# Stick-breaking and sliding-window units in turns of two: one layer of a hybrid decoder

## The chip, the cores and the metric

The kernel runs on one core of one Trainium2 chip. The metric is the device time of one execution in microseconds. Before the change it is 1794.3 us, the median of 3 runs (1792.6 to 1796.31). The profile comes from one further execution of the same program.

## The reference

One layer over 1024 positions with a model width of 2048. A pre-norm, one input projection to 6656 columns, two groups of attention heads side by side, and one output projection:

```
u = rmsnorm(x, norm_pre)
q_sb, k_sb, v_sb, z_sb, q_sw, k_sw, v_sw, z_sw = split(u @ w_in)
# stick-breaking, 16 heads of 64, s < t:
w[t,s] = sigmoid(l[t,s]) * prod_{s<j<t} (1 - sigmoid(l[t,j]));   l = q.k / 8
# sliding window of 128, 16 query heads on 4 key/value heads, bias by distance, one sink logit per head:
p = softmax over the window and the sink
y = concat(rmsnorm(o_sb) * silu(z_sb), rmsnorm(o_sw) * silu(z_sw)) @ w_out
out = x + rmsnorm(y, norm_post)
```

Everything is float32. The kernel keeps that precision by splitting an operand into a rounded part and a remainder ("h" and "l" in the names) and adding up two or three matmuls.

## The kernel before

The input projection is cut into 52 blocks of 128 columns. Three of them are computed while x is loaded; the others follow in the order of the list `work`, each by `proj`: 16 contraction tiles, three matmuls of 128x512 per tile and half of the positions, 96 "long" matmuls in a block (tiles p_..., line 122). The weights of a block come in four parts (`split_w`, lines 128 to 136): a load, a rounding on ScalarE (whi) and a subtraction on VectorE (wlo), one part ahead of its use.

The attention is cut into units, which are put between the long matmuls. After every three long matmuls of a contraction tile `proj` calls `step`, and `advance` decides whether something of a unit is issued. A unit has three stages on TensorE, all "small" matmuls:

- s1: the logits, four matmuls of 128x256 into a bank of PSUM (tile z_..., two buffers). ScalarE, GpSimd and VectorE then make the weights: for a stick-breaking unit two sigmoids (lines 555 and 557), two scans (565 or 568) and a product (571) into b_sb; for a sliding-window unit bias, maximum, exponentials, sum and scaling (639 to 654) into L_sw.
- s2: up to four 128x128 transposes of these weights (tile wt_..., line 126, two buffers), which ScalarE rounds (wh_..., lines 586 and 665) and VectorE subtracts (wl_..., 587 and 666).
- s3: up to four matmuls of 128x256 with the values (tile o_...). There is one PSUM buffer for it (`po`, lines 91 and 92). ScalarE copies a finished output to ot_... (line 518), from where it is stored.

A pair of stick-breaking heads (names sb0 to sb7) has 20 units, ten a head: query blocks a = 0 to 3, and for each the key blocks c = a to 3, which add up into one output; only the unit with c = 3 is followed by a copy. A group of sliding-window heads (sw0 to sw3) has 16 units, and each has an output and a copy of its own. In the names, sb2_0_1_3 is pair 2, head 0, a = 1, c = 3; sw1_5_0 is group 1, block 5, first two heads.

`pe_time` adds up the nominal time of all matmuls issued so far. Units wait in `todo` until a period has passed since the last start (4.7 or 3.8 us); a unit's s2 is due 6.2 or 7.0 us after its s1 was issued, its s3 4.5 or 5.0 us after its s2. When a period has passed, `advance` issues, in this order: all outputs that are due, one start (s1), and one s2; s2 goes ahead of the start where three units are already begun. When no unit is left to start, outputs and transposes are issued one by one as they come due. The order of TensorE's instructions is kept as the program writes it; the order on the other engines comes from a scheduler.

When a block of values is finished (`done_vsw`, `done_v_sb`), `drain` forces all units of earlier heads that use the value tiles, then `evac_v` takes two value tiles (tag "v", two buffers) and puts off the transposes of the values (vt_..., line 414) by 4 or 9 us; the next head's units are offered 6 us later.

After the attention the output projection runs as seven products of half-size matrices with sums (lines 935 to 994), in which no unit takes part.

Of the kernel before, what the change touches and what calls it, by code (L numbers as in the profile page):

```python
# [12 lines left out]
F32R = mybir.dt.float32r  # L13
# [6 lines left out]
P = 128  # L20
# [37 lines left out]
def layer(ctx, tc, xT, x, w_first, w_blk, w_out, g_pre, g_post, g_sb, g_sw, sinks, rel, onehot, penalty, out):  # L58
# [29 lines left out]
    def pw(name, shape=None):  # L88
        return ptile("pw", name, 2, shape)
# [62 lines left out]
    def advance(force=False):  # L152
        now = pe_time[0]
        while waiting and (force or waiting[0][0] <= now):
            todo.extend(waiting.pop(0)[1])
            prep()
        if later and (force or later[0][0] <= now):
            later.pop(0)[1]()
            return True
        if force or not todo:  # L160
            return finish_stage2(force, now) or finish_stage1(force, now) or (bool(todo) and start(now))
        if len(stage1) - stage1_due(now) < todo[0]["depth"] and last_start[0] + todo[0]["period"] <= now:
            while finish_stage2(False, now):
                pass
            late = len(stage1) >= todo[0]["depth"]
            if late:
                finish_stage1(False, now)
            begun = start(now)
            if not late:
                finish_stage1(False, now)  # L170
            return begun
        return False

    def start(now):
# [8 lines left out]
        prep()  # L183
        return True

    def stage1_due(now):
        return 1 if stage1 and len(stage2) < 3 and stage1[0][0] + stage1[0][1]["lag"] <= now else 0

    def finish_stage2(force, now):
        if stage2 and (force or stage2[0][0] + stage2[0][1]["lag2"] <= now):  # L190
            u = stage2.pop(0)[1]
# [3 lines left out]
        return False  # L195

    def finish_stage1(force, now):
        if stage1 and len(stage2) < 3 and (force or stage1_due(now)):
# [325 lines left out]
    def units_sb(pair, vst):  # L524
        units = []
        for hh in range(2):
            row = hh * HD
            head = {}
            for a in range(4):
                grp = {}  # L530
                for c in range(a, 4):
                    units.append(unit_sb(pair, hh, row, a, c, head, grp, vst[hh]))
        return units

    def unit_sb(pair, hh, row, a, c, head, grp, vs):
        nm = f"sb{pair}_{hh}_{a}"
        un = f"{nm}_{c}"
        me = {}
# [51 lines left out]
        def s3():  # L590
            if c == a:
                grp["o"] = po(f"o_{nm}")
            for j in range(2):
                for i, wt in enumerate(me["wt"]):
                    mm(grp["o"][:, :256], vs[:, 2 * c + j, :], wt[:, 2 - 2 * j:4 - 2 * j, :],
                       start=(c == a and j == 0 and i == 0), stop=(c == 3 and j == 1 and i == 1))
            if c == 3:
                finish_o(grp["o"], nm, pair, row, slice(a * 256, (a + 1) * 256))
# [10 lines left out]
    def unit_sw(g, i, hp, head, vg):  # L609
# [59 lines left out]
        def s3():  # L669
            ops = po(f"o_{un}")  # L670
            for j in range(nj):
                for r, wt in enumerate(me["wt"]):
                    mm(ops[:, :256], vg[:, i + j, :], wt[:, j, :],
                       start=(j == 0 and r == 0), stop=(j == nj - 1 and r == 1))
            finish_o(ops, un, 8 + blk, None, slice(i * P, (i + 1) * P))

# [14 lines left out]

    def done_vsw(i):
        def f(ps):
            for g in range(2 * i):
                drain(f"sw{g}")
            vs["sw", 2 * i], vs["sw", 2 * i + 1] = evac_v(ps, f"vsw{i}", 4.0 if i else 9.0)
        return f

    def done_q_sb(p):
# [4 lines left out]

    def done_v_sb(p):
        def f(ps):
            for g in range(4):
                drain(f"sw{g}")
# [332 lines left out]
```

## Time and profile before

| | |
|---|---|
| median of 3 runs | 1794.3 us (1792.6 to 1796.31) |
| the profiled execution's own time | 1794.37 us |
| its span, first to last instruction | 1792.5 us |
| mean granted clock of TensorE | 0.998 |
| TensorE matmuls (PE), busy | 1770.6 us, 9046 instructions |
| VectorE (DVE), busy | 1230.5 us |
| ScalarE (ACT), busy | 784.4 us |
| GpSimd (POOL), busy | 497.2 us |

PE is TensorE, PEld its weight loads, SP the engine that issues most DMAs. Times are microseconds unless marked ns. In a row of the timeline stand the start, the length, the engine, the line and operation, out<-in by the program's names without numbers, and the shapes; in brackets the idle time before it and what ended it. In a row of the waits stand the waiting engine, its tile and line, what it waited for, and then the sum, the number of waits and the longest. In a row of the groups stand the count (x...), the busy time, the mean length in ns, and the idle time before them with what ended it. Matmuls overlap and their ends are modelled, so their starts tell more than their lengths.

### The profile page before, as it was taken

The page shows a single profiled execution, that of the slowest core. Times are in us where ns is not written, and L with a number is a line of the kernel's source. Part 1 is how long each engine was busy: PE and PEld are TensorE (multiplying, and loading weights), DVE is VectorE, ACT ScalarE, POOL GpSimd, SP SyncE. Part 2 cuts the span into 40 slices and gives each one's busy share as a digit, 9 for nine tenths or more (in the row PEclk, how much of TensorE's full clock was granted, in tenths as well). Part 3 has the DMA queues.
Part 4 walks back from the last instruction along what each step waited for, and adds up shares of the span by engine and source line. Part 5 has one row for each costly group of instructions (what it writes and reads, how often), then busy time and mean ns, then how long its engine had stood idle before and what let it go on. Part 6 is the DMA issues. An engine that isn't in the chain of part 4 may idle for free. (4 is left out here: it accounts for less than half of the span.)

```text
span 1792.5 us, 27351 instructions
## 1 busy us (share of the span) xinstructions
PE 1770.6 (99%) x9046; PEld 1500.1 (84%) x9046; DVE 1230.5 (69%) x1984; ACT 784.4 (44%) x1696; POOL 497.2 (28%) x648
## 2 busy tenths in 40 slices
PE   8999999999999999999999999999999999999998
PEld 7788888888888888888888888888888887888886
DVE  7567842678367688675785777767868646855795
ACT  7345531456344444343443444444434434444442
POOL 0012121211213334233233332232313224504533
PEclk9999999999999999999999999999999999999999
DMA  7557775566746656556456563454434385634484
GB/s 232 191 162 212 211 223 158 163 205 204 222 134 182 181 168 190 162 182 183 156 166 178 177 181 124 154 164 142 146 106 136 103 256 190 210 100 140 136 286 155
DMA packets 203884, 312.48 MB, mean 174 GB/s; under 512 B 24640, under 2 KB 84192, under 8 KB 203616
## 3 DMA queue, kind: packets, MB, share of 16 engines
q1 hardware_dynamic: 201680, 307.60, 55.8%
q10 hardware_dynamic: 2064, 3.15, 0.5%
q8 instruction: 72, 1.18, 0.3%
q14 instruction: 68, 0.56, 0.1%
HBM read 219.42 MB, written 91.23 MB: 173 GB/s over the span
## 5 line engine op out<-in xcount | busy, mean ns | idle before, releaser
L587 DVE TENSOR_TENSOR wl_sb<-wt_sb,wh_sb 128x512 fp32r<-128x512 f32 (+1 forms) x160 | 100.7, 633 | 95.8 <-ACT wh_sb L586 95.8
L571 DVE TENSOR_TENSOR b_sb<-b_sb,m_sb 128x512 f32<-128x512 f32 x160 | 129.2, 807 | 42.1 <-POOL b_sb L561 19.1
L586 ACT CAST wh_sb<-wt_sb 128x512 fp32r<-128x512 f32 (+1 forms) x160 | 87.0, 544 | 136.3 <-PE wt_sb L126 134.3
L568 DVE TENSOR_TENSOR_SCAN m_sb<-m_sb,m_sb,zero 128x257 f32<-128x257 f32 x192 | 143.4, 785 | 2.4 <-ACT m_sb L555 2.1
L933 PE MATMUL y<-wohi,x 128*128 128x512 f32 x448 | 141.9, 393 | 1.5 <-ACT wohi L797 1.5
L933 PE MATMUL y<-wohl,x 128*128 128x512 f32 x576 | 132.5, 389 | 0.0
L933 PEld LDWEIGHTS y<-wohl,x 128*128 128x128 f32 x576 | 108.1, 188 | 22.4
L565 DVE TENSOR_TENSOR_SCAN m_sb<-m_sb,mask 128x256 f32<-128x256 f32 x128 | 119.8, 972 | 5.8 <-ACT m_sb L555 5.8
L648 ACT ACTIVATE L_sw<-L_sw,nm_sw 128x256 f32<-128x256 f32 (+1 forms) x128 | 63.1, 494 | 93.1 <-DVE nm_sw L643 91.7
L122 PE MATMUL p_vsb<-xh,whi_vsb 128*128 128x512 f32 x256 | 102.0, 398 | 0.0
L933 PEld LDWEIGHTS y<-wohi,x 128*128 128x128 f32 x448 | 84.9, 189 | 19.9 <-ACT wohi L797 1.9
L122 PE MATMUL p_ksb<-xh,wlo_ksb 128*128 128x512 f32 x256 | 100.7, 393 | 0.0
L122 PE MATMUL p_qsb<-xh,whi_qsb 128*128 128x512 f32 x256 | 100.6, 393 | 0.0
L122 PE MATMUL p_zsw<-xh,wlo_zsw 128*128 128x512 f32 x256 | 100.6, 393 | 0.0
L122 PE MATMUL p_qsb<-xh,wlo_qsb 128*128 128x512 f32 x256 | 100.6, 393 | 0.0
L122 PE MATMUL p_vsb<-xh,wlo_vsb 128*128 128x512 f32 x256 | 100.5, 393 | 0.0
L122 PE MATMUL p_ksb<-xl,whi_ksb 128*128 128x512 f32 x256 | 100.5, 392 | 0.0
L122 PE MATMUL p_vsb<-xl,whi_vsb 128*128 128x512 f32 x256 | 100.4, 392 | 0.0
L122 PE MATMUL p_qsb<-xl,whi_qsb 128*128 128x512 f32 x256 | 100.4, 392 | 0.0
L122 PE MATMUL p_zsw<-xl,whi_zsw 128*128 128x512 f32 x256 | 100.4, 392 | 0.0
L122 PE MATMUL p_zsb<-xh,wlo_zsb 128*128 128x512 f32 x256 | 100.4, 392 | 0.0
L122 PE MATMUL p_zsb<-xl,whi_zsb 128*128 128x512 f32 x256 | 100.2, 391 | 0.0
(243 smaller groups left out, 4988.3 us busy)
## 6 DMA issues: line engine op xcount, KB each, us to landing
row_sw<-in_w_out SPq DMA_DIRECT2D x80, 256.0 KB, 4.3
bg<-in_w_out SPq DMA_DIRECT2D x80, 256.0 KB, 4.3
woraw<-wsum SPq DMA_DIRECT2D x80, 256.0 KB, 3.4
kh<-kd SPq DMA_DIRECT2D x160, 64.0 KB, 2.9
kl<-kd SPq DMA_DIRECT2D x160, 64.0 KB, 2.4
wsum<-row_sw SPq DMA_DIRECT2D x40, 256.0 KB, 2.9
wsum<-bg SPq DMA_DIRECT2D x40, 256.0 KB, 3.3
q_sw<-qd SPq DMA_DIRECT2D x64, 128.0 KB, 3.5
```

Source lines behind the costliest of these rows:

```text
L122: tc.keep_in_program_order(nc.tensor.matmul(ps, a, b, start=start, stop=stop))
L565: nc.vector.tensor_tensor_scan(m[:, tb, 1:257], m[:, tb, 1:257], mask[:, P - P * tb:P - P * tb + 256], m[:, tb, 0:1], ALU.mult, ALU.max)
L568: nc.vector.tensor_tensor_scan(m[:, tb, :], m[:, tb, :], zero.to_broadcast([P, 257]), prev[:, tb, 256:257], ALU.mult, ALU.max)
L571: nc.vector.tensor_mul(beta, beta, m[:, :, 0:256])
L586: nc.scalar.copy(wh[:, :k], pt[:, :k])
L587: nc.vector.tensor_sub(wl[:, :k], pt[:, :k], wh[:, :k].bitcast(F32))
L648: nc.scalar.activation(L[:, hh, :n], L[:, hh, :n], AF.Exp, bias=nm[:, hh:hh + 1], accum_out=sm[:, hh:hh + 1])
L933: nc.tensor.matmul(ps, xt[:, a, tcols], w[b][:, cols], start=first and n == 0, stop=last and n == 2)
```

## The change

`advance` now works in turns of two units. When two periods have passed since the last start, it issues: one output that is due; up to two s2 that are due; up to two starts; and then all other outputs that are due. The test on the number of units begun before a turn is gone (`start` still refuses a fourth), and `stage1_due` with it. `drain` calls the outputs, the transposes and the starts itself, instead of `advance`. And the draining of earlier heads moves from the end of a value block into the put-off work of `evac_v`: it is done, and the value tiles are taken, when the first value transposes are due. For that, units get the list of value tiles or a function instead of the tile.

```diff
-        if len(stage1) - stage1_due(now) < todo[0]["depth"] and last_start[0] + todo[0]["period"] <= now:
+        if last_start[0] + 2 * todo[0]["period"] <= now:
+            finish_stage2(False, now)
+            turned = finish_stage1(False, now) and finish_stage1(False, now)
+            begun = start(now) and (not todo or start(now))
             while finish_stage2(False, now):
                 pass
-            late = len(stage1) >= todo[0]["depth"]
-            if late:
-                finish_stage1(False, now)
-            begun = start(now)
-            if not late:
-                finish_stage1(False, now)
-            return begun
+            return begun or turned
         return False
...
     def drain(key):
         n = left.get(key, 0)
         while left.get(key, 0):
-            assert advance(True)
+            assert finish_stage2(True, pe_time[0]) or finish_stage1(True, pe_time[0]) or start(pe_time[0])
...
-    def evac_v(ps, name, lag=4.0):
-        vst = [at.tile([P, 8, P], F32R, tag="v", name=f"v_{name}_{j}") for j in range(2)]
+    def evac_v(ps, name, ended=(), lag=4.0):
+        vst = []
         us = [scaled(ps[h], name, h) for h in range(2)]
 
         def finish(h):
+            if h == 0:
+                for key in ended:
+                    drain(key)
+                vst.extend(at.tile([P, 8, P], F32R, tag="v", name=f"v_{name}_{j}") for j in range(2))
...
     def done_v_sb(p):
         def f(ps):
-            for g in range(4):
-                drain(f"sw{g}")
-            drain(f"sb{p - 1}")
-            offer(6.0, f"sb{p}", units_sb(p, evac_v(ps, f"vsb{p}")))
+            ended = [f"sw{g}" for g in range(4)] + [f"sb{p - 1}"]
+            offer(6.0, f"sb{p}", units_sb(p, evac_v(ps, f"vsb{p}", ended)))
```

What this does to the order, at three places. First TensorE in sliding-window group 1, from the output of block 4 to that of block 5 (o_ are outputs, wt_ transposes, z_ logits, p_qsb0 long matmuls of a projection). Before, with twelve long matmuls between two turns:

```order
L122 MATMUL o_sw1_4_0_2438<-wh_sw1_4_0_2350,v_vsw0_1_833 128x256
...
L126 MATMUL wt_sw1_6_0_2446<-ident_190,L_sw1_6_0_2302 128x128 x4
L122 MATMUL z_sw1_1_1_2455<-kh_1065,q_sw1_0_1_2265 128x256
...
L122 MATMUL p_qsb0_0_2217<-xh8_408,whi_qsb0_2_2330 128x512
...
L122 MATMUL p_qsb0_0_2217<-xh11_523,wlo_qsb0_2_2332 128x512
L122 MATMUL o_sw1_5_0_2496<-wh_sw1_5_0_2399,v_vsw0_1_833 128x256
...
L126 MATMUL wt_sw1_7_0_2504<-ident_190,L_sw1_7_0_2359 128x128 x2
L122 MATMUL z_sw1_2_1_2511<-kh_1065,q_sw1_2_1_2374 128x256
```

And now, one turn between two long matmuls of the same projection:

```order
L122 MATMUL p_qsb0_1_2132<-xh14_643,wlo_qsb0_3_2317 128x512
L122 MATMUL o_sw1_3_0_2488<-wh_sw1_3_0_2338,v_vsw0_1_916 128x256
...
L126 MATMUL wt_sw1_6_0_2496<-ident_190,L_sw1_6_0_2347 128x128 x4
L122 MATMUL z_sw1_1_1_2505<-kh_1065,q_sw1_0_1_2278 128x256
...
L122 MATMUL o_sw1_4_0_2528<-wh_sw1_4_0_2394,v_vsw0_1_916 128x256
...
L122 MATMUL o_sw1_5_0_2536<-wh_sw1_5_0_2403,v_vsw0_1_916 128x256
...
L122 MATMUL p_qsb0_1_2132<-xh15_692,whi_qsb0_3_2315 128x512
```

The outputs of blocks 4 and 5 now stand directly behind each other, and that of block 3 opens the same turn. The four groups have 16 such pairs without a matmul between; in the order before there is none. Two periods of 3.8 us are shorter than the lag of a second unit begun in the turn before, so in these groups a turn with three outputs and one start alternates with a turn of two transposes and two starts, 30 and 9 long matmuls apart.

Next TensorE in stick-breaking pair 2, around the unit a = 2, c = 2 of the first head. Before, its transposes stand three turns behind its logits:

```order
L122 MATMUL z_sb2_0_2_2_8399<-kh_1065,q_sb2_0_2_8244 128x256
...
L122 MATMUL z_sb2_0_2_3_8466<-kh_1065,q_sb2_0_2_8244 128x256
...
L122 MATMUL z_sb2_0_3_3_8516<-kh_1065,q_sb2_0_2_8244 128x256
...
L122 MATMUL o_sb2_0_1_8502<-wh_sb2_0_1_2_8462,v_vsb2_0_7997 128x256
...
L126 MATMUL wt_sb2_0_2_2_8559<-ident_190,b_sb2_0_2_2_8406 128x128 x3
```

And now:

```order
L122 MATMUL z_sb2_0_2_2_8411<-kh_1065,q_sb2_0_2_8313 128x256
...
L122 MATMUL o_sb2_0_1_8491<-wh_sb2_0_1_1_8383,v_vsb2_0_8028 128x256
...
L126 MATMUL wt_sb2_0_2_2_8505<-ident_190,b_sb2_0_2_2_8418 128x128 x3
L122 MATMUL z_sb2_0_2_3_8515<-kh_1065,q_sb2_0_2_8313 128x256
...
L122 MATMUL z_sb2_0_3_3_8532<-kh_1065,q_sb2_0_2_8313 128x256
...
L122 MATMUL o_sb2_0_1_8491<-wh_sb2_0_1_2_8394,v_vsb2_0_8028 128x256
```

The transposes of the unit now stand in the next turn, which also starts two units; 33 long matmuls lie between two turns.

Last VectorE at the same place (m_sb are scans, b_sb products, wl_sb the remainders of the transposes, wlo the remainder of a projection's weights). Before:

```order
L568 SCALAR_TENSOR_TENSOR m_sb2_0_1_3_8356<-m_sb2_0_1_3_8356,m_sb2_0_1_2_8310,zero_204 128x257 x2
L571 TENSOR_TENSOR b_sb2_0_1_3_8358<-b_sb2_0_1_3_8358,m_sb2_0_1_3_8356 128x512
L587 TENSOR_TENSOR wl_sb2_0_1_1_8394<-wt_sb2_0_1_1_8389,wh_sb2_0_1_1_8393 128x384
L565 SCALAR_TENSOR_TENSOR m_sb2_0_2_2_8404<-m_sb2_0_2_2_8404,mask_206 128x256 x2
L571 TENSOR_TENSOR b_sb2_0_2_2_8406<-b_sb2_0_2_2_8406,m_sb2_0_2_2_8404 128x512
L135 TENSOR_TENSOR wlo_zsw4_3_8439<-wraw_zsw4_3_8435,whi_zsw4_3_8437 128x512
```

And now:

```order
L585 TENSOR_TENSOR wl_sb2_0_1_1_8384<-wt_sb2_0_1_1_8379,wh_sb2_0_1_1_8383 128x384
L585 TENSOR_TENSOR wl_sb2_0_1_2_8395<-wt_sb2_0_1_2_8389,wh_sb2_0_1_2_8394 128x512
L566 SCALAR_TENSOR_TENSOR m_sb2_0_1_3_8403<-m_sb2_0_1_3_8403,m_sb2_0_1_2_8321,zero_204 128x257 x2
L569 TENSOR_TENSOR b_sb2_0_1_3_8405<-b_sb2_0_1_3_8405,m_sb2_0_1_3_8403 128x512
L563 SCALAR_TENSOR_TENSOR m_sb2_0_2_2_8416<-m_sb2_0_2_2_8416,mask_206 128x256 x2
L135 TENSOR_TENSOR wlo_zsw4_3_8450<-wraw_zsw4_3_8446,whi_zsw4_3_8448 128x512
L569 TENSOR_TENSOR b_sb2_0_2_2_8418<-b_sb2_0_2_2_8418,m_sb2_0_2_2_8416 128x512
```

The work of two units now stands in one piece: two remainders, then scans and product of the first unit, then those of the second, with a weight remainder ahead of the second product. (The lines of the changed kernel are smaller by up to six: 565 is 563 there.)

More of the change, by code (lines that the diff above doesn't have):

```diff
@@ L184, in start @@
         return True
-    def stage1_due(now):
-        return 1 if stage1 and len(stage2) < 3 and stage1[0][0] + stage1[0][1]["lag"] <= now else 0
     def finish_stage2(force, now):
@@ L197, in finish_stage1 @@
     def finish_stage1(force, now):
-        if stage1 and len(stage2) < 3 and (force or stage1_due(now)):
+        if stage1 and len(stage2) < 3 and (force or stage1[0][0] + stage1[0][1]["lag"] <= now):
             u = stage1.pop(0)[1]
@@ L531, in units_sb, with unit_sb @@
                 for c in range(a, 4):
-                    units.append(unit_sb(pair, hh, row, a, c, head, grp, vst[hh]))
+                    units.append(unit_sb(pair, hh, row, a, c, head, grp, vst))
         return units
-    def unit_sb(pair, hh, row, a, c, head, grp, vs):
+    def unit_sb(pair, hh, row, a, c, head, grp, vst):
         nm = f"sb{pair}_{hh}_{a}"
@@ L594, in s3 @@
                 for i, wt in enumerate(me["wt"]):
-                    mm(grp["o"][:, :256], vs[:, 2 * c + j, :], wt[:, 2 - 2 * j:4 - 2 * j, :],
+                    mm(grp["o"][:, :256], vst[hh][:, 2 * c + j, :], wt[:, 2 - 2 * j:4 - 2 * j, :],
                        start=(c == a and j == 0 and i == 0), stop=(c == 3 and j == 1 and i == 1))
@@ L672, in s3 @@
                 for r, wt in enumerate(me["wt"]):
-                    mm(ops[:, :256], vg[:, i + j, :], wt[:, j, :],
+                    mm(ops[:, :256], vg()[:, i + j, :], wt[:, j, :],
                        start=(j == 0 and r == 0), stop=(j == nj - 1 and r == 1))
@@ L693, in f @@
         def f(ps):
-            for g in range(2 * i):
-                drain(f"sw{g}")
-            vs["sw", 2 * i], vs["sw", 2 * i + 1] = evac_v(ps, f"vsw{i}", 4.0 if i else 9.0)
+            vst = evac_v(ps, f"vsw{i}", [f"sw{g}" for g in range(2 * i)], 4.0 if i else 9.0)
+            for j in range(2):
+                vs["sw", 2 * i + j] = lambda j=j: vst[j]
         return f
@@ L706, in f @@
         def f(ps):
-            for g in range(4):
-                drain(f"sw{g}")
-            drain(f"sb{p - 1}")
-            offer(6.0, f"sb{p}", units_sb(p, evac_v(ps, f"vsb{p}")))
+            ended = [f"sw{g}" for g in range(4)] + [f"sb{p - 1}"]
+            offer(6.0, f"sb{p}", units_sb(p, evac_v(ps, f"vsb{p}", ended)))
         return f
```

## The prediction

> **What bounds the kernel now.** I read the page first, for the share of each engine and its course over the span; then the chain of waits of TensorE, for the time in which it stands still; then its timeline, for the distance from the start of one matmul to the start of the next, because the busy time of matmuls that overlap does not add up. The page's first lines:
>
> ```profile
> span 1792.5 us, 27351 instructions
> PE 1770.6 (99%) x9046; PEld 1500.1 (84%) x9046; DVE 1230.5 (69%) x1984; ACT 784.4 (44%) x1696; POOL 497.2 (28%) x648
> PE   8999999999999999999999999999999999999998
> ```
>
> TensorE is busy in every slice but the first and the last. Nothing that only moves work of other engines can save time, unless it shortens the stream of matmuls or one of its waits. The waits of TensorE, longest first:
>
> ```profile
> PE f0a L122 <- ACT whi_f L332: 5.8, 1, 5.8
> PE o_sb L122 <- ACT ot_sb L518: 3.1, 3, 1.4
> PE wt_sb L126 <- DVE wl_sb L587: 1.6, 1, 1.6
> PE y L933 <- ACT wohi L797: 1.5, 1, 1.5
> PE o_sw L122 <- ACT ot_sw L518: 1.3, 4, 0.5
> PE y L933 <- DVE wolo L798: 0.3, 1, 0.3
> ```
>
> The first belongs to the start and the two of y to the output projection; the change reaches neither. In the attention part, where it works, TensorE waits 3.1 + 1.6 + 1.3 = 6.0 us in eight places, seven of them for ScalarE's copy out of the one PSUM bank of an output ("po", one buffer). These waits are counted from a matmul's modelled end, so the loss is a little larger: here the last long matmul begins at 1080.12 and the output at 1081.65, 1.53 us later instead of 0.23, so 1.30 us are lost where the row says 1.15.
>
> ```profile
> 1080.12 0.39 PE L122 MATMUL p_vsb<-xh,wlo_vsb 128*128 128x512 f32 x1
> 1081.65 0.36 PE L122 MATMUL o_sb<-wh_sb,v_vsb 128*128 128x256 f32 x1 [1.15 <-ACT ot_sb L518]
> ```
>
> With 0.15 to 0.17 more in each of eight places, some 7.4 us are all that the old waits can give back. The rest of the attention is a full stream, and there a second, smaller loss shows. Nine long matmuls in an undisturbed stretch (the first two rows; eight starts left out between them), and nine that follow a turn of small ones (the other rows):
>
> ```profile
> 615.28 0.39 PE L122 MATMUL p_zsw<-xh,whi_zsw 128*128 128x512 f32 x1
> ...
> 617.32 0.39 PE L122 MATMUL p_zsw<-xh,whi_zsw 128*128 128x512 f32 x1
> ```
>
> ```profile
> 803.24 0.28 PE L122 MATMUL z_sb<-kh,q_sb 128*128 128x256 f32 x1
> 803.36 0.28 PE L122 MATMUL z_sb<-kl,q_sb 128*128 128x256 f32 x1
> 803.48 0.39 PE L122 MATMUL p_zsw<-xh,whi_zsw 128*128 128x512 f32 x1
> ...
> 805.56 0.39 PE L122 MATMUL p_zsw<-xh,whi_zsw 128*128 128x512 f32 x1
> ```
>
> 617.32 - 615.28 = 2.04 us, or 0.227 a matmul; 805.56 - 803.48 = 2.08 us. An interruption costs 0.04 us behind it, apart from its own small matmuls (0.12 us each).
>
> **The change part by part.** No instruction is added or removed on TensorE; the order alone changes.
>
> *Fewer interruptions.* In the order of before, small matmuls break the stream of projections 324 times, 235 times with nine or more long matmuls behind and 89 times with three or six. In the order now it is 203: 146 and 57. At 0.04 us each, and half of it (chosen between nothing and all) where the run is too short: before 9.4 + 1.8 = 11.2, now 5.8 + 1.2 = 7.0. Gain 4.2 us; 3.6 with nothing for the short ones, 4.8 with 0.04 for all.
>
> The Trainium skill ("TensorE: Matmul & The Clock Gate", section "Back-to-back issue gap") gives for an isolated warm matmul a distance that depends on its own columns alone, with no price for a neighbour of another size; by that this gain would be nothing and my forecast 4.2 us higher. The rows above disagree, so the sum keeps the 4.2.
>
> *Two outputs in a row.* This is the term that decides. A sliding-window unit has an output of its own, so each output waits until ScalarE has copied the one before out of the only bank. Before, outputs stood a period apart. Now a turn opens with one output, and where a turn ends with two, the second stands directly behind the first: 16 places in the four sliding-window groups, and one at the very end of the last stick-breaking head. What the bank needs between two outputs, the trace shows where they came close and ScalarE was idle:
>
> ```profile
> 240.42 0.28 PE L122 MATMUL o_sw<-wl_sw,v_vsw 128*128 128x256 f32 x1
> ...
> 240.78 0.37 ACT L518 COPY ot_sw<-o_sw 128x256 f32<-128x256 f32 x1 [1.27 <-PE o_sw L122]
> ...
> 241.24 0.36 PE L122 MATMUL o_sw<-wh_sw,v_vsw 128*128 128x256 f32 x1
> ```
>
> 0.82 us from the last matmul of one output to the first of the next, of which 0.12 is the matmul's own: 0.70 us lost. At another place the copy took 0.41 us to the next output's start instead of 0.46, which makes 0.65:
>
> ```profile
> 202.92 0.35 ACT L518 COPY ot_sw<-o_sw 128x256 f32<-128x256 f32 x1
> ...
> 203.33 0.39 PE L122 MATMUL o_sw<-wh_sw,v_vsw 128*128 128x256 f32 x1 [0.28 <-ACT ot_sw L518]
> ```
>
> I take 0.67: 17 x 0.67 = 11.4 us, and 0.2 each for two places where only a logit block stands between (0.59 us of matmuls): 11.8 us. Ends: 17 x 0.65 = 11.1 and 17 x 0.70 + 0.5 = 12.4. Nothing covers it: TensorE takes its instructions in order and the projections stand behind the second output.
>
> *The other close outputs.* At the head ends the last outputs come three long matmuls after each other (3 x 0.227 + 0.12 = 0.80 us, 17 places), and 16 turns have 1.0 us between the opening output and the first closing one. With ScalarE idle, 0.82 us are enough, so these cost next to nothing. But a copy that stands behind exponentials comes late: at 203.33 it began behind them. The three o_sb waits (3.1 us) say 1 us where it happens; between never and one place in three lies 0 to 0.35 a place. I take 0.12, one place in eight, as most old copies made nobody wait: 33 x 0.12 = 4 us, ends 0 and 11.6.
>
> *The old waits.* Sliding-window turns and head ends are laid out anew, so I take all 7.4 us away; their successors are the term above. If half of them stay, it is 3.7.
>
> *VectorE's burst.* A stick-breaking turn now starts two units, whose transposes stand one turn later. Behind the second unit's logits come an output (0.48), 33 long matmuls (7.5), an output (0.48) and the first unit's transposes (three take 0.30 below): the second unit's weights are due 8.9 us later. Before, it was three turns, each with 15 or 18 long matmuls, about 14 us.
>
> ```profile
> 837.92 0.55 PE L126 MATMUL wt_sb<-ident,b_sb 128*128 128x128 f32 x3 [1.61 <-DVE wl_sb L587]
> 838.22 0.48 PE L122 MATMUL p_vsb<-xh,whi_vsb 128*128 128x512 f32 x1
> ```
>
> ```profile
> L568 DVE TENSOR_TENSOR_SCAN m_sb<-m_sb,m_sb,zero 128x257 f32<-128x257 f32 x192 | 143.4, 785 | 2.4 <-ACT m_sb L555 2.1
> L571 DVE TENSOR_TENSOR b_sb<-b_sb,m_sb 128x512 f32<-128x512 f32 x160 | 129.2, 807 | 42.1 <-POOL b_sb L561 19.1 <-POOL m_sb L559 9.5 <-ACT whi_zsb L133 0.5
> L587 DVE TENSOR_TENSOR wl_sb<-wt_sb,wh_sb 128x512 fp32r<-128x512 f32 (+1 forms) x160 | 100.7, 633 | 95.8 <-ACT wh_sb L586 95.8
> L565 DVE TENSOR_TENSOR_SCAN m_sb<-m_sb,mask 128x256 f32<-128x256 f32 x128 | 119.8, 972 | 5.8 <-ACT m_sb L555 5.8
> L135 DVE TENSOR_TENSOR wlo_zsw<-wraw_zsw,whi_zsw 128x512 fp32r<-128x512 f32 x32 | 26.9, 840 | 12.5 <-ACT whi_zsw L133 6.3 <-PE o_sb L122 5.3 <-PE vt_vsb L126 0.6
> ```
>
> VectorE's row of such a turn: two wl (1.27), two scans of each kind (1.57 + 1.94), two products (1.61) and one foreign instruction, a weight split (0.84): 7.2 us. The first wl can begin some 0.6 us before the logits end, so the second unit is ready after 6.6 us, with 2.3 to spare. That holds unless VectorE itself waits, as it does for GpSimd:
>
> ```profile
> DVE b_sb L571 <- POOL b_sb L561: 19.1, 8, 4.3
> DVE b_sb L571 <- POOL m_sb L559: 9.5, 3, 3.4
> ```
>
> Eleven waits of 2.6 us on average: 0.3 over what is to spare, 3.3 us; I take 3. Ends: 0, and 8 if a third of them run to the 4.3 of the longest.
>
> *Heads end when the next values are due.* The forced end of a head moves from the projection's end to four microseconds of matmuls later, and the value tiles are taken then. In both orders a head's last units come out in their own time before it, so hardly anything is left to force, and I cost it at nothing; what hides it is the six microseconds of matmuls that lie between a projection and its first logits, and without them a forced unit would wait for VectorE as at 837.92, 1.6 us a head. The output projection's order is the same as before.
>
> *The sum.* -4.2 + 11.8 + 4 - 7.4 + 3 = +7.2 us. It is made against the profiled execution, 1794.4 us (span 1792.5 and 1.9 around it), which equals the median of the three runs shown, 1794.3: **1801.6 us**, 0.4% slower. A measurement of this kernel tells about 0.2%, or 3.6 us, from no change: 1790.7 to 1797.9 is "same".
>
> **The rivals.**
>
> *All else is covered (same).* The near outputs and VectorE's burst cost nothing; then -4.2 + 11.1 - 7.4 = -0.5: 1793.9, and up to 1797 with a little of either. For it: ScalarE is busy 44% and idle before the copy at 240.78. Against: seven of the eight old waits were copies that came late. 0.18, and a part of my own forecast's case reaches below 1797.9 as well (0.07).
>
> *Double outputs are cheap (faster).* If the second output's weights are in place and the copy overlaps the first output's last matmuls, the wait falls to 0.25 us or less; from there the gains win: -4.2 - 7.4 + 17 x 0.25 = -7.4: 1787. Against it stands the row at 241.24, the same two instructions with an idle ScalarE. 0.10.
>
> *The burst comes late (slower still).* VectorE's instructions stretch at times: of two weight splits that the same stretch of its timeline shows, one takes 1.78 us and one 0.69.
>
> ```profile
> 789.13 1.78 DVE L135 TENSOR_TENSOR wlo_zsw<-wraw_zsw,whi_zsw 128x512 fp32r<-128x512 f32 x1
> ...
> 796.83 0.69 DVE L135 TENSOR_TENSOR wlo_zsw<-wraw_zsw,whi_zsw 128x512 fp32r<-128x512 f32 x1
> ```
>
> Two or three stretched instructions use up the 2.3 us. If a third of the 70 full turns lose 0.8 us, that is 19 us in place of my 3: 1818. Against: the means above hold these long ones already. 0.12.
>
> *The clock falls.* The stretch after the wait of y runs slow:
>
> ```profile
> 1482.00:1485.40 3.40, 3.40 (x11) 2.67 (x10) 1.32 (x2) 0.97 (x2) 2.00 (x2) 0.55 0.83 265
> ```
>
> A granted clock of 0.55 over 3.4 us costs 1.5 us. If every double output brought this on, 17 x 1.5 = 26 more: 1827. Against: the 1.61 us wait at 837.92 is followed by the next start after 0.30, as fast as elsewhere. 0.05. The Trainium skill ("TensorE: Matmul & The Clock Gate", section "A second HAM failure mode: psum-queue depth-cycling") tells of this mechanism, short idle times between groups that cycle through PSUM; in the attention part this trace shows none of it.
>
> **How the numbers follow.** My case has 0.55, the rivals 0.18, 0.10, 0.12 and 0.05. Faster 0.10; same 0.18 + 0.07 = 0.25; slower 0.65. My case alone runs from 1793.2 (all ends low: -4.8 + 11.1 - 7.4) to 1819 (-3.6 + 12.4 + 11.6 - 3.7 + 8), and its tails are thin. Leaving out the clock, most of the faster case and the upper part of the late burst, 0.2 together, the range is 1791.5 to 1816.
>
> **What would show it.** In TensorE's waits, o_sw for ScalarE's ot_sw should rise from 1.3 us in 4 to some 7 to 10 us in 16 or more, each about half a microsecond beyond the modelled end. Nine long matmuls behind a turn should still take 2.08 us. Waits of wt_sb for VectorE should be few and short; more than 10 us of them makes the burst the cause. If o_sw's waits stay under 3 us, the central step is wrong. If the waits add up but the time does not, the 0.04 is.

## The result, and the profile after

The changed kernel takes 1817.3 us, the median of 6 runs (1810.7 to 1818.9), against 1794.6 before: a ratio of 1.0123, with a 95% interval from 1.0109 to 1.0138. It is slower, as forecast, but by 22.6 us where 7.2 were forecast, and 1.3 us outside the range. The profiled execution took 1814.0 us, 19.6 more than the one profiled before; it lies 3.3 us under its median, and the working below is made on it. The engines on its page, whose span is 1812.3 us:

```profile
PE 1776.6 (98%) x9046; PEld 1502.5 (83%) x9046; DVE 1242.1 (69%) x1984; ACT 774.0 (43%) x1696; POOL 508.8 (28%) x648
```

The same 9046 matmuls. The busy time of TensorE has hardly grown; the span has, by waits. The longest of them:

```profile
PE o_sw L122 <- ACT ot_sw L516: 11.2, 21, 1.7
PE f0a L122 <- ACT whi_f L326: 5.7, 1, 5.7
PE p_vsb L122 <- DVE wlo_vsb L135: 3.1, 2, 3.0
PE wt_sb L126 <- DVE b_sb L569: 2.8, 5, 1.6
PE y L929 <- ACT wohi L793: 1.8, 1, 1.8
PE o_sb L122 <- ACT ot_sb L516: 1.6, 2, 1.0
```

The first row is the one that the prediction named, and a little above the size that it named (7 to 10 us, 16 times or more): outputs of sliding-window units that wait for ScalarE's copy. The third is of a kind that was not there before: a long matmul of a projection waits for the remainder of its weights.

Counted from start to start (the distance from one matmul's start to the next, less the undisturbed distance of its kind, 0.227 us for a long one, 0.118 or 0.119 for a logit or output, 0.109 for a transpose; what is over by more than 0.06 us counts as a wait), the two traces compare so:

| us lost on TensorE | before | after |
|---|---|---|
| outputs of sliding-window units | 2.6 | 17.6 |
| outputs of stick-breaking units | 4.0 | 4.5 |
| transposes late from VectorE | 2.1 | 3.8 |
| long matmuls late from VectorE | 0 | 4.8 |
| starts at half the clock, in the attention | 0 | 1.8 |
| behind interruptions, up to 0.06 us each | 10.7 | 6.4 |
| other small ones | 0.6 | 1.2 |

The sums are 20.0 and 40.1; their difference, 20.1, is within 0.3 us of that of the spans, 19.8. The first matmul of the output projection begins at 1473.2 before and at 1492.8 after, so the loss lies ahead of it.

What a pair of outputs costs, in the changed kernel's timeline (TensorE and ScalarE):

```profile
152.56 0.28 PE L122 MATMUL o_sw<-wl_sw,v_vsw 128*128 128x256 f32 x1
...
152.88 0.37 ACT L516 COPY ot_sw<-o_sw 128x256 f32<-128x256 f32 x1 [0.55 <-PE o_sw L122]
...
153.31 0.39 PE L122 MATMUL o_sw<-wh_sw,v_vsw 128*128 128x256 f32 x1 [0.46 <-ACT ot_sw L516]
...
153.53 0.28 PE L122 MATMUL o_sw<-wl_sw,v_vsw 128*128 128x256 f32 x1
```

From 152.56 to 153.31 are 0.75 us where 0.12 would do, and the next matmul follows after 0.22 where 0.12 would do: 0.73 lost. There are 17 such pairs, 12.5 us.

In another turn the copy of the opening output stands in ScalarE's queue behind the exponentials (L_sw) of the units that the turn before began and behind a weight rounding (whi):

```profile
193.23 0.28 PE L122 MATMUL z_sw<-kl,q_sw 128*128 128x256 f32 x1
...
193.74 0.49 ACT L646 ACTIVATE L_sw<-L_sw,nm_sw 128x256 f32<-128x256 f32 x1
...
194.32 0.60 ACT L133 CAST whi_qsb<-wraw_qsb 128x512 fp32r<-128x512 f32 x1
...
194.83 0.36 ACT L516 COPY ot_sw<-o_sw 128x256 f32<-128x256 f32 x1
...
195.24 0.39 PE L122 MATMUL o_sw<-wh_sw,v_vsw 128*128 128x256 f32 x1 [1.73 <-ACT ot_sw L516]
...
196.44 0.38 PE L122 MATMUL o_sw<-wh_sw,v_vsw 128*128 128x256 f32 x1 [0.46 <-ACT ot_sw L516]
```

1.9 us are lost at 195.24 and 0.6 at 196.44, and then the clock falls. Two windows of the changed kernel, the turn's end and what follows (the column behind the five engines is the granted clock):

```profile
195.20:197.00 1.80, 1.30 (x7) 1.09 (x8) 1.73 (x6) 0.84 (x2) 0.75 (x1) 0.93 0.72 248
197.00:200.40 3.40, 3.40 (x10) 2.60 (x9) 2.74 (x7) 1.13 (x4) 0.00 (x0) 0.54 0.42 108
```

### The profile page after: what moved, and what is told of

Same layout as the page of the kernel before. It is cut to its first block, busy times and chain, and to the rows that moved or that the text cites. A ratio compares the mean times of both kernels' runs of the same rounds, so it can differ in the third digit from the quotient of the medians.

```text
span 1812.3 us, 27295 instructions
## 1 busy us (share of the span) xinstructions
PE 1776.6 (98%) x9046; PEld 1502.5 (83%) x9046; DVE 1242.1 (69%) x1984; ACT 774.0 (43%) x1696; POOL 508.8 (28%) x648
## 5 line engine op out<-in xcount | busy, mean ns | idle before, releaser
L585 DVE TENSOR_TENSOR wl_sb<-wt_sb,wh_sb 128x512 fp32r<-128x512 f32 (+1 forms) x160 | 97.0, 634 | 127.6 <-ACT wh_sb L584 127.3
L584 ACT CAST wh_sb<-wt_sb 128x512 fp32r<-128x512 f32 (+1 forms) x160 | 81.6, 546 | 151.5 <-PE wt_sb L126 150.8
L563 DVE TENSOR_TENSOR_SCAN m_sb<-m_sb,mask 128x256 f32<-128x256 f32 x128 | 130.1, 1045 | 4.9 <-ACT m_sb L553 2.6
L569 DVE TENSOR_TENSOR b_sb<-b_sb,m_sb 128x512 f32<-128x512 f32 x160 | 124.6, 779 | 9.8 <-POOL b_sb L559 3.9
L929 PEld LDWEIGHTS y<-wohi,x 128*128 128x128 f32 x448 | 84.8, 189 | 20.1 <-ACT wohi L793 2.2
L122 PE MATMUL p_zsw<-xh,whi_zsw 128*128 128x512 f32 x256 | 100.1, 391 | 0.1
L122 PE MATMUL p_ksb<-xh,whi_ksb 128*128 128x512 f32 x256 | 100.0, 390 | 0.0
```

Source lines behind the costliest of these rows:

```text
L122: tc.keep_in_program_order(nc.tensor.matmul(ps, a, b, start=start, stop=stop))
L563: nc.vector.tensor_tensor_scan(m[:, tb, 1:257], m[:, tb, 1:257], mask[:, P - P * tb:P - P * tb + 256], m[:, tb, 0:1], ALU.mult, ALU.max)
L569: nc.vector.tensor_mul(beta, beta, m[:, :, 0:256])
L584: nc.scalar.copy(wh[:, :k], pt[:, :k])
L585: nc.vector.tensor_sub(wl[:, :k], pt[:, :k], wh[:, :k].bitcast(F32))
L929: nc.tensor.matmul(ps, xt[:, a, tcols], w[b][:, cols], start=first and n == 0, stop=last and n == 2)
```

## The experiments

**Theory 1** says that the loss is outputs that wait for their one buffer, above all in the sliding-window turns. **Theory 2**, the rival, says that it is VectorE, on which two stick-breaking units now come at once. The expectations were written ahead of each run. In brackets behind a time stands the ratio to the runs of before that were made beside it, with its 95% interval; it is worked out from all runs and need not equal that of the two medians.

**One half of the change at a time.** Turns of two for one kind of unit, and ahead of them, for the other kind ("sw" or "sb"), the old test and the old body of a turn; and the later end of heads alone.

```diff
+        if todo[0]["key"][:2] == "sw":
+            if len(stage1) - stage1_due(now) >= todo[0]["depth"] or last_start[0] + todo[0]["period"] > now:
+                return False
...
```

> The changed kernel with turns of two for the stick-breaking units alone; sliding-window units take turns of one as before. Theory 1, outputs: the 17.6 us of o_sw and the 1.8 us of half clock go, some 2.6 us of the old waits of o_sw come back and 24 more interruptions cost 1 us; some 16 us less than the changed kernel, 1799 to 1803. Theory 2, VectorE's burst: the loss lies in the stick-breaking part and stays, 1810 or more.

Measured: 1800.1 us (12 runs; ratio to before 1.0031, 1.0020 to 1.0043).

> The changed kernel with turns of two for the sliding-window units alone; stick-breaking units take turns of one as before. Theory 1, outputs: the time before, with 17.6 us of waiting outputs and 1.8 us of half clock, less 2.6 us of old waits and 1 us of interruptions: some 16 us above before, 1808 to 1812. Theory 2, VectorE's burst: no stick-breaking turn starts two units, so at most 4 us above before, 1795 to 1799.

Measured: 1808.1 us (6 runs; 1.0071, 1.0052 to 1.0090).

> The kernel before with the other part of the change alone: heads are forced to their end, and the value tiles taken, when the first value transposes are due. TensorE's order has the same number of interruptions and the same distances between outputs as before. Both theories: within 0.2% of before, 1791 to 1798; a third way, that the later taking of the value tiles delays the copies of the values, would cost 2 us or more at each of ten value blocks, 1800 or more.

Measured: 1793.4 us (12 runs; 0.9998, 0.9986 to 1.0010).

The sliding-window half costs 13.1 us over its own runs of before (1795.0), the stick-breaking half 5.0, the heads' end nothing. Both times the result lies in the range of theory 1, but the stick-breaking half was forecast to gain: the terms of the prediction that lie in it are -3.6 for interruptions (its trace shows 10.7 falling to 7.1), +0.7 for the pair at the end of the last head, +2 for 17 close outputs, +3 for VectorE and some -5 for old waits, together -3. It costs 5. Its waits:

```profile
PE o_sb L122 <- ACT ot_sb L531: 4.7, 3, 2.4
PE p_vsb L122 <- DVE wlo_vsb L135: 3.1, 1, 3.1
```

Of the three old waits of o_sb one has gone, but the two at the end of the fifth pair of heads have grown from 1.8 to 4.1 us (the third of the row is the new pair, 0.6), and a wait of a long matmul has come. The parts make 18.1 us together, the whole 22.6. The other 4.5 are not clear of noise: the intervals of the three ratios together allow 4.8 us (estimated from their halves, 3.4, 2.1 and 2.6).

**The outputs' buffer.** Three ways to take the wait between two outputs away. First, they alternate between the halves of the bank, each 256 of its 512 columns:

```diff
+        obank[1] += 1
+        return obank[0][:, obank[1] % 2 * 256:obank[1] % 2 * 256 + 256]
...
-            ops = po(f"o_{un}")
+            ops = po_half(f"o_{un}")
```

> The changed kernel, with outputs alternating between the two halves of the one PSUM bank, so that an output does not wait for the copy of the one before. Order of the matmuls unchanged. Theory 1, the outputs on one buffer: in the changed kernel's trace the starts of outputs come 22.1 us late in all (o_sw 17.6, o_sb 4.5), and 1.8 us more of half clock follow two of these waits; nearly all of it goes, and the time falls by 20 to 24 us, to 1793 to 1797. Theory 2, VectorE's burst: most of the loss comes from weights and remainders that VectorE delivers late; the outputs' waits only move behind those, and the time falls by less than 8 us, to 1809 or more. A third way: TensorE cannot write one half of a bank while ScalarE reads the other; then nothing changes, 1815 to 1819, and the waits on the copy stay under a new name.

Measured: 1815.4 us (5 runs; 1.0111, 1.0090 to 1.0132), the third way. The wait is there under its new name:

```profile
PE obank L122 <- ACT ot_sw L524: 12.5, 22, 1.8
```

In the program that was built, the first matmul of an output still waits for the semaphore count of the copy of the other half (0.46 us at 153.66 in its trace, as at 153.31 in the changed kernel's), so the run never took the wait away and tells nothing of theory 1. What the bank itself would have done is not shown by it. The Trainium skill ("PSUM — Partial Sum Buffer", section "PSUM bank collisions raise a hardware error") says that two engines that touch the same partitions of one bank at once collide, in disjoint columns too, and that the guard is to go by the bank and not by the address; no run here shows a collision, and the wait in this program goes by the bank.

Second, both outputs at a turn's end go into the two halves, and both copies come after both (`finish_o`, which issues the copy, at first only notes the output in `ends`):

```diff
+            together[0] = True
             while finish_stage2(False, now):
                 pass
+            together[0] = False
+            assert len(ends) < 3
+            while ends:
+                finish_o(*ends.pop(0))
```

> The changed kernel; the outputs at a turn's end go into the two halves of the bank, and both copies come after both outputs, so that the program has no wait between the two. The first of them still waits for the copy of the output that opened the turn. Theory 1, outputs on one buffer: the 16 waits between the two outputs (0.62 us and 0.10 more at the first matmul behind each, 11.5 us) go, with them most of the 1.8 us of half clock: 1803 to 1807. Theory 2, VectorE's burst: the sliding-window pairs don't matter, 1813 or more.

Measured: 1809.1 us (6 runs; 1.0086, 1.0066 to 1.0105), 8.2 less than the changed kernel (by the two ratios 6.6), 2 above the range of theory 1 and 4 below that of theory 2. Its row of the waits:

```profile
PE obank L122 <- ACT ot_sw L532: 7.9, 8, 1.7
```

The pairs' waits are gone (from start to start, sliding-window outputs behind another output lost 12.7 us in the changed kernel and lose 1.3 here), but the first output of a pair now waits longer for the copy of the opening one (behind a logit block: 3.5 before this edit, 8.3 with it). So a part of the wait that was removed came back in the one ahead of it.

Third, an output at a turn's end stands back until 1.2 us of matmuls (GAP) lie behind the one before, else it comes at a later step:

```diff
-            while finish_stage2(False, now):
-                pass
+            rest[0] = sum(at + u["lag2"] <= now for at, u in stage2)
+            spaced(now)
...
+        while rest[0] and last_o[0] + GAP <= pe_time[0] and finish_stage2(False, now):
```

> The changed kernel; an output at a turn's end is issued only when 1.2 us of matmuls lie behind the one before, else after the next three or six long matmuls. No pair stands directly together any more, none is nearer than 0.8 us; 36 interruptions more. Theory 1, outputs on one buffer: o_sw's 17.6 us and the 1.8 us of half clock go, 1.4 us come for the interruptions, 1797 to 1803, about where turns of two for the stick-breaking units alone stand (1800.1). Theory 2, VectorE's burst: 1813 or more.

Measured: 1807.7 us (6 runs; 1.0079, 1.0060 to 1.0098): 9.6 less, 5 above the range. Outputs of sliding-window units lose 8.9 us instead of 17.6, and 7.4 of it in six places, one of 3.6: there the copy is late by ScalarE's queue, and distance between outputs does not help.

**GpSimd.** VectorE's lateness has a place in the changed kernel that shows how it comes about (GpSimd, VectorE, and the long matmul at the end):

```profile
606.60 1.29 POOL L434 TENSOR_TENSOR or_zsw<-or_zsw 128x512 f32<-128x512 f32 x1 [9.20 <-DMA or_zsw<-od]
...
607.92 0.62 POOL L559 TENSOR_SCALAR_AFFINE_SELECT b_sb<-b_sb 128x512 f32<-128x512 f32 x1
607.93 1.16 DVE L449 TENSOR_TENSOR u_zsw<-u_zsw,or_zsw 128x512 f32<-128x512 f32 x1 [2.49 <-POOL m_sb L557]
...
609.01 1.77 DVE L569 TENSOR_TENSOR b_sb<-b_sb,m_sb 128x512 f32<-128x512 f32 x1
...
610.71 2.39 DVE L563 TENSOR_TENSOR_SCAN m_sb<-m_sb,mask 128x256 f32<-128x256 f32 x2
...
613.02 0.66 DVE L135 TENSOR_TENSOR wlo_vsb<-wraw_vsb,whi_vsb 128x512 fp32r<-128x512 f32 x1
...
613.73 0.79 PE L122 MATMUL p_vsb<-xh,wlo_vsb 128*128 128x512 f32 x1 [2.97 <-DVE wlo_vsb L135]
```

GpSimd stands 9.2 us for a load of finished outputs, whose two parts it then adds up for the gate (or_zsw, line 434). VectorE's next instruction is the gate's product (u_zsw, line 449), which reads this sum; VectorE waits 2.5 us for it. (The row names m_sb, a small GpSimd instruction just behind the sum.) Behind the product stand b_sb, which takes 1.77 us beside a GpSimd addition, the scans of the second unit, and only then the projection's weight remainder. So two things come together here, the wait for the sum and the long instruction. The next runs ask about the second: they cut GpSimd's background additions (sums of output weights, of which each is 128x512) to 16 columns:

```diff
-            BG((nc.gpsimd.tensor_add if sign > 0 else nc.gpsimd.tensor_sub)(t[:, 0, :], t[:, 0, :], t[:, 1, :]))
+            BG((nc.gpsimd.tensor_add if sign > 0 else nc.gpsimd.tensor_sub)(t[:, 0, :16], t[:, 0, :16], t[:, 1, :16]))
```

> The changed kernel with GpSimd's background additions of the output weights cut to 16 of 512 columns (so the summed weights are not computed in full; the DMAs, the waits and the order stay). The theory that VectorE is late because its instructions are stretched beside GpSimd's additions: the waits of TensorE for VectorE in the attention part, 8.2 us (wt_sb 3.6, weight remainders 4.2, others), fall under 3 us, and the time by 4 to 7 us, 1810 to 1813. The rival, that two units at a time are too much for VectorE by themselves: the waits stay at 7 us or more and the time above 1815.

Measured: 1803.9 us (6 runs; 1.0059, 1.0042 to 1.0076), 13.4 less than the changed kernel (by the two ratios 11.5), more than the 4 to 7 of the theory, and far from its rival. TensorE's waits for VectorE in the attention fall from 6.2 us to 2.5 in the rows, under 3 as the theory has it. Those of the transposes go; the long one stays in part:

```profile
PE p_vsb L122 <- DVE wlo_vsb L135: 2.2, 2, 2.1
```

At its place b_sb now takes 0.70 us instead of 1.77, but VectorE waits as long as before, 2.6 us, for the gate's sum. So of the 3.0 us of this wait 0.9 came from the background addition, and the other 2.1 did not.

> The kernel before with the same cut of GpSimd's background additions. Both theories: TensorE waits 1.8 us for VectorE there, so at most 3 us are to be had, 1791 to 1796; more would mean that the additions also cost TensorE time in another way.

Measured: 1783.7 us (5 runs; 0.9944, 0.9929 to 0.9959), 10.7 less than before. Not expected: in the kernel before nearly every wait of the attention part goes.

```profile
PE o_sw L122 <- ACT ot_sw L518: 0.4, 1, 0.4
...
PE wt_sb L126 <- DVE wl_sb L587: 0.2, 1, 0.2
```

So the additions delayed ScalarE's copies too, not only VectorE; by which way is not shown. But the difference between the two kernels is hardly touched: 20.3 us with the cut, 22.6 without. Little of the change's cost, if any, comes from the background additions. One more run asks that of the stick-breaking half:

> Turns of two for the stick-breaking units alone, with GpSimd's background additions cut to 16 of 512 columns (the summed weights are not computed in full). Without the cut, turns of two for these units cost 5.0 us over before (1800.1 against 1795.0); the kernel before with the cut takes 1783.7. Theory A, the cost of these turns is VectorE and ScalarE held up by GpSimd's additions, which two units at a time can bear less: with the cut the 5 us go and the fewer interruptions show, 1780 to 1784. Theory B, the burst of two units costs by itself: 1787 to 1790.

Measured: 1789.3 us (8 runs; 0.9966 of before, 0.9953 to 0.9979): 5.6 above the kernel before with the same cut, or 4.0 by the two ratios, each to its own runs of before (5.6 without the cut, reckoned in the same way). Theory B: within the noise the half costs by itself what it cost with the additions. Its waits:

```profile
PE o_sb L122 <- ACT ot_sb L531: 2.9, 3, 1.7
PE p_vsb L122 <- DVE wlo_vsb L135: 1.9, 1, 1.9
PE p_zsb L122 <- DVE wlo_zsb L135: 1.3, 1, 1.3
```

No transposes among them: the units are in time, the projection and the outputs are late. What the longest of each kind have in common is the gate. Ahead of the remainder that is late by 1.9 us, VectorE waits 2.5 us for a sum of the gate in this run too. And the output that is late by 1.7 us waits for a copy that stands behind ScalarE's square (acc_sb) of another such sum (GpSimd, ScalarE, and TensorE):

```profile
1075.78 1.27 POOL L449 TENSOR_TENSOR or_zsb<-or_zsb 128x512 f32<-128x512 f32 x1 [1.00 <-DMA or_zsb<-od]
...
1077.08 0.63 ACT L467 ACTIVATE acc_sb<-or_zsb 128x512 f32<-128x512 f32 x1 [6.18 <-POOL m_sb L572]
1077.62 0.35 ACT L531 COPY ot_sb<-o_sb 128x256 f32<-128x256 f32 x1
...
1078.12 0.35 PE L122 MATMUL o_sb<-wh_sb,v_vsb 128*128 128x256 f32 x1 [1.71 <-ACT ot_sb L531]
```

ScalarE stands 6.2 us; at the same output it stood 4.9 us before the change (1080.62) and 5.5 in the changed kernel (1098.90). No run moved these sums or their loads, so that a good part of the half's cost hangs on them is read from the traces and not shown by an experiment. Whether the weight remainder would be in time if it were made two parts ahead was not tried either.

**A version that beats both.** The cut shows what is to be had in the kernel before. Two ways to have it with the whole result; first the same background work (these additions, and two other GpSimd operations beside them, not printed here) in pieces of 128 columns, before and with the stick-breaking half:

```diff
+            for c in range(0, HALF, P):
+                BG((nc.gpsimd.tensor_add if sign > 0 else nc.gpsimd.tensor_sub)(
+                    t[:, 0, c:c + P], t[:, 0, c:c + P], t[:, 1, c:c + P]))
```

> The kernel before, the whole result computed, with each background operation of GpSimd in pieces of 128 columns instead of 512 or 1024, so that GpSimd does as much, but in shorter instructions. Theory A1, VectorE's instruction with two inputs in SBUF stands still until the GpSimd instruction beside it has ended: it then stands for a quarter of the time at most, and a part of the 10.7 us that the cut gave comes without the cut, 1786 to 1791. Theory A2, what costs is how long GpSimd is busy in all, because other work stands behind its additions: no gain, 1793 or more.

Measured: 1792.1 us (9 runs; 0.9982, 0.9971 to 0.9992), 3.1 less than the 17 runs of before beside it (1795.2): a small gain, between A1 and A2.

> Turns of two for the stick-breaking units alone, the whole result computed, with GpSimd's background operations in pieces of 128 columns. Theory A1: the 5.0 us that these turns cost go at least by half, 1786 to 1793, at best below the kernel before in pieces. Theory A2 or B: no change from 1800.1, 1798 to 1802.

Measured: 1801.6 us (5 runs; 1.0032, 1.0020 to 1.0044): nothing, as theory B has it. Pieces make GpSimd busier. The groups of these additions, before and in pieces:

```profile
L251 POOL TENSOR_TENSOR row_sw<-row_sw 128x512 f32<-128x512 f32 x40 | 56.8, 1421 | 125.4 <-DMA row_sw<-in_w_out 125.3
```

```profile
L252 POOL TENSOR_TENSOR row_sw<-row_sw 128x128 f32<-128x128 f32 x160 | 85.6, 564 | 121.5 <-DMA row_sw<-in_w_out 121.4
```

A quarter of the columns takes 0.56 us, not a quarter of 1.42. Second, of the 80 sums the 48 with a plus sign are made by the second load itself, 8 us after the first; the other 32 stay in pieces as above:

```diff
-            BG(nc.sync.dma_start(t[:, 1, :], w_view(b, e, cols)))
+            if sign < 0:
+                BG(nc.sync.dma_start(t[:, 1, :], w_view(b, e, cols)))
             yield 8.0
...
+            if sign > 0:
+                BG(nc.gpsimd.dma_start(t[:, 0, :], w_view(b, e, cols), accum_op=ALU.add))
```

> The kernel before, the whole result computed; of the 80 background sums the 48 with a plus sign are made by a DMA that GpSimd issues and that adds to what it finds, the rest in pieces of 128 columns as in the run before. Theory: what TensorE loses to GpSimd's background additions (10.7 us, of which the pieces gave back 2.9) goes in proportion to the additions taken away, 1786 to 1790. The rival: GpSimd is held as long by issuing such a DMA or by waiting for the first one to land, and nothing is gained over the pieces, 1791 or more.

Measured: 1785.2 us (5 runs, 1785.0 to 1786.7; 0.9955, 0.9942 to 0.9969), 8.6 less than before, 0.8 below the range expected, and 32 less than the changed kernel. The pieces alone gave 3.1. No wait for VectorE is left in the attention part, and one row for the outputs:

```profile
PE o_sw L122 <- ACT ot_sw L525: 0.6, 2, 0.4
```

## Why the prediction was right and wrong

The sign was right, the size was not. The sum was short by 12.4 us on the profiled execution, and two terms make up 11.2 of it: the other close outputs (+4, measured 9.6) and VectorE's burst (+3, measured 8.6). Term by term:

- **What bounds the kernel.** Right: no instruction came or went on TensorE, and the time moved by its waits alone.
- **Fewer interruptions, -4.2.** Right: 10.7 fell to 6.4, -4.3. Behind a turn nine long matmuls still take 2.08 us (782.03 - 779.95, eight starts left out):

```profile
779.95 0.39 PE L122 MATMUL p_zsw<-xh,whi_zsw 128*128 128x512 f32 x1
...
782.03 0.39 PE L122 MATMUL p_zsw<-xh,whi_zsw 128*128 128x512 f32 x1
```

  The Trainium skill's distance that depends on a matmul's own columns alone ("TensorE: Matmul & The Clock Gate", section "Back-to-back issue gap"), which the prediction weighed, has no place for these 0.04 us; the trace does not agree with it.
- **Two outputs in a row, +11.8.** Right in mechanism and size: 17 pairs cost 12.5 us. "Nothing covers it" holds as well, and taking these waits away gave 8.2 us.
- **The other close outputs, +4.** Wrong in size: the 22.1 us of outputs less the pairs leave 9.6. "With ScalarE idle, 0.82 us are enough, so these cost next to nothing" holds well enough: the outputs three long matmuls apart lost about 0.1 each, 1.5 us in 16 places. The step that failed is "one place in eight": how often a copy is late, and by how much, was taken from before. A turn that starts two units also gives ScalarE two units' sigmoids or exponentials at once, and the copies of this turn and the next stand behind them (194.83 above). About half of the 9.6 us was lost behind logit blocks, most of it in three of the 16 turns (2.0, 0.9 and 0.7 us); the rest were single late copies.
- **The old waits, -7.4.** Right but for 1.5 us: from start to start 8.7 us were there. Only the two outputs at the end of the fifth pair of heads wait again, 1.5 us together where they lost 2.4; the rest of o_sb's 4.5 is new. The same two cost 4.5 in the stick-breaking half alone, nothing with short additions in the kernel before and in the changed one, and 2.6 in the half with short additions. So they hang on the layout as well as on the additions.
- **VectorE's burst, +3.** Wrong, and by as much: 8.6 us. That the second unit is ready in time ("after 6.6 us, with 2.3 to spare") holds, as transposes lose but 3.8. (The 8.9 us from which this is reckoned are 8.8 with the 0.30 named for the transposes.) But the prediction asked only when the units are due. The burst also stands ahead of an instruction for somebody else, the projection's weight remainder, and its 4.8 us were in no term and no rival, although the order in the section on the change shows this instruction behind the first unit's product and the second's scans. And "unless VectorE itself waits" was priced by its waits for masks; the wait that mattered, 2.5 us ahead of 607.93, was for a sum of the gate.
- **The clock.** The rival had the place right and the size wrong. It was to cost 1.5 us at every double output; it came behind two long waits (195.24 and 613.73). In this trace slow starts make the 1.8 us of the table's row and about 1.1 more, behind 613.73, that it counts under long matmuls and outputs. In the six runs the mean granted clock is 0.9958, in 23 runs of before 0.9980. Taken over 1816 us that would be 4.0 us, which is an upper bound: the two profiled executions differ about as much (0.996 against 0.998), and a part of their slow stretches lies where TensorE has nothing left to do (a granted clock of 0.69 from 1805 us to the end). About 3 us is what the starts show.
- **Heads' end, 0.** Right: 0.9998, 0.9986 to 1.0010. **The output projection** unchanged: right, its stretch differs by 0.1 us.

The new waits were forecast at 18.8 us and came to 32.5 by the table (17.6 + 4.5 + 3.8 + 4.8 + 1.8); with 8.7 of old ones gone and 4.3 won, that leaves 19.5. The rival "the burst comes late" gave 1818, near the result, but by luck: it had 19 us of late transposes, and the trace shows 3.8. What stays open is whether the whole costs more than its parts, what the gate's sums cost, by which way the background additions delay ScalarE, and why the clock fell behind two waits and not behind others as long: at 837.92 before, 1.6 us of wait left it at 1.00 from 837.9 to 841.

## What to carry to other kernels

Grouping small work between long matmuls wins little per interruption (0.04 us here), and hands every other engine its work in lumps: before doing it, list what else stands in the queues behind the lump, not only when the lump itself is due. A buffer of one is paid in full where two users come together, and a wait that is taken away is given in part to the next wait ahead of it. Cutting a background job to a stub, in the old kernel too, is a cheap way to see what it costs: here it found 10.7 us that none of the engines' busy shares pointed to. And read what the instruction that waits itself reads, not only the name in the brackets: here it led from the units' masks to the gate.

## What the runs showed of the hardware

A matmul that waited is followed more slowly: 0.22 us to the next instead of 0.12 (153.31 to 153.53 above). TensorE's weight load begins at 153.31 too, together with its matmul, so no weights were loaded ahead when the wait ended.

VectorE instructions with two inputs in SBUF can stand still beside a GpSimd one (changed kernel, GpSimd and VectorE):

```profile
1196.81 2.84 POOL L256 TENSOR_TENSOR bg<-bg,row_sw 128x1024 f32<-128x1024 f32 x1
...
1197.31 2.89 DVE L569 TENSOR_TENSOR b_sb<-b_sb,m_sb 128x512 f32<-128x512 f32 x1
```

The product takes 2.89 us and ends 0.55 behind the GpSimd instruction; alone it takes 0.69. Over the trace of before, the median of these products is 1.53 us in 32 places beside a GpSimd instruction of 0.9 us or more, and 0.69 in the 128 others; the remainders of transposes, which read one input from PSUM, take 0.69 in both. It matters which of the two begins first: in the 21 of these 32 places where GpSimd did, the product takes 1.1 to 2.7 us and ends 0.55 us behind it; in the 11 where VectorE did, it takes 0.69. In the changed kernel it takes 1.5 us or more in nine of ten places where GpSimd began first, and at most 1.05 in the 31 where VectorE did. The Trainium skill ("SBUF — State Buffer", section "Who interferes with whom") says that a VectorE instruction with two SBUF inputs contends with a GpSimd instruction that reads SBUF, and calls the pair of ports that they share an exclusive lock. The trace agrees. The prediction saw such an instruction (1.78 us at 789.13) and left its cause open.

In the last run, accumulating loads issued by GpSimd did the additions of 48 blocks, and TensorE's waits show none for them.
